# Attention heads that take the first half of the sequence before the second, in a one-core decoder block

## The chip, the core and the metric

The kernel runs on one core of a Trainium2 chip. Its engines have queues of their own and wait for each other by semaphores: TensorE (PE, with its weight loads shown as PEld), VectorE (DVE), ScalarE (ACT), GpSimd (POOL) and SyncE (SP), which here only issues DMAs. The metric is the time of one execution on the device in microseconds; less is better.

## The reference

One layer, sequence 1024, width 1024, all float32. Two token mixers share one input projection; their outputs are gated, added and projected, and a SwiGLU channel mixer follows.

```python
h = rms_norm(x, attn_norm_w)
q, k, v, u, g = split(h @ w_in)             # 1024 + 1024 + 1024 + 2048 + 2048 columns
q, k = rms_norm(q per 64), rms_norm(k per 64)   # 8 heads, two halves of 64 each
# per head, blocks of 128 rows of q:
p = softmax(q1 k1^T / 8 + bias, causal) - lam * softmax(q2 k2^T / 8 + bias, causal)
a = rms_norm(p @ v, subln_w) * (1 - lam_init)
c = silu(layer_norm(causal_conv31(u_a * sigmoid(u_b))))
x = x + (sigmoid(g_a) * (a @ w_proj_attn) + sigmoid(g_b) * (c @ w_proj_conv)) @ w_out
x = x + (silu(gate(rms_norm(x))) * up(rms_norm(x))) @ w_down
```

## The kernel before

Every float32 product is made of three passes (`mm3`, L168 to L170): each operand is split into a rounded part (`hi`, a cast on ACT, L120) and a rest (`lo`, a subtraction on DVE, L125). The kernel runs in stages: the opening with the first projections, the rest of the `u` projections (with the convolution's taps started on DVE), attention, the two output projections, `w_out`, and the channel mixer.

The change lies in **attention**, and in the step that makes q and k for it.

`q_item(h)` projects q and k of head h. It does so in two halves of the sequence, `b` = 0 for rows 0 to 511 and `b` = 1 for rows 512 to 1023. For each half two groups of 48 matmuls fill a PSUM bank each (`pg`), ACT copies them and sums the squares, DVE scales them; later `turn_qk` transposes the half (tile `pQ`, L815), splits it into parts (`ks`, `klo`, `qs`) and moves 64 partitions about with small DMAs on SP (L826 to L837). Each turn waits in the list `late` with a number, `free`: the step before which it may not run, since its buffers are still read.

Attention is a loop over 64 **steps** (h, i): head h, row block i of 128 queries. `ORDER` gives the row blocks' order in a head. A step does this:

- `scores(h, i)`: block i needs (i+1)*128 keys. For each of the two softmaxes PE makes score tiles `sc` of at most 512 keys (L1289, L1290; three PSUM buffers). DVE adds the bias `tb` and finds the minimum (L1291), which frees the buffer; ACT takes the exponential with its sum (L1296); DVE combines the two softmaxes into one tile `E` (L1303 to L1306). Block 7 therefore costs eight times block 0.
- `more`: one group of other work for PE, from `fill`: the projections of the next head's q and k ("Q", four groups a head) and of the gates ("G", two groups each), 24 matmuls of 512 columns or 48 of 256. This is what PE does while DVE and ACT work on the scores. In heads with six groups, two steps have none.
- `turn` of the step before: PE transposes `E` (tile `pT`, L1328), ACT and DVE split it into `ph`, `pl`.
- `slot`: after each second block, `weigh` multiplies by v (tile `pW`, `vh`, `vl`), `back` and `subln` finish the rows (tiles `pB`, `an`, `pS`), and turns of q and k that are due run.
- the convolution's remaining taps (L594, about 1.26 us each on DVE), dealt out by a rough estimate of how much longer PE is busy in a step than DVE (`slack_of`); the last two steps get none of it.

The bias tile `tb` and the v tiles have one buffer each. `tb` of the next head is loaded when the last scores of a head have been read (L869), v of the next head when its last `weigh` has run (L1265).

After the scores of the last step three groups of G are left, which stand over the end of attention: the last `turn`, `weigh`, `back`, `subln`, and the reloading of finished heads (`early`, L1492) for the projection of the attention output, which follows with `aT_hi`, `aT_lo` as its operands.

The instructions of each engine are not issued in the order in which they are written: a scheduler moves them, within rules such as `after(...)`, so that groups of other work come early where it expects PE to wait. `more` lets a group come at most about three steps early.

Of the kernel before, what the change touches and what calls it, by code (L numbers as in the profile page):

```python
# [19 lines left out]
H = 8  # L20
# [11 lines left out]
NT = S // P  # L32
# [25 lines left out]
def kernel(  # L58
# [53 lines left out]
    def nm(s):  # L112
        uid[0] += 1
        return f"{s}_{uid[0]}"

    def f32(ap):
        return ap.bitcast(F32)
# [36 lines left out]
    def pg():  # L154
        npg[0] += 1
        p_, tag = pgs[npg[0] % len(pgs)]
        return p_.tile([P, 512], F32, tag=tag, name=nm("pg"))
# [4 lines left out]
    def pm(z="pm"):  # L162
        npm[0] += 1
        p_, tag = pms[npm[0] % len(pms)]
        return p_.tile([P, 512], F32, tag=tag, name=nm(z))
# [86 lines left out]
    def pcol(key, k=0):  # L252
        c = col[key] + k
        return pvec[:, c : c + 1]
# [121 lines left out]
    def gemm_N(o, halves, shi, slo, i):  # L376

        ts = slice(i * P, (i + 1) * P)
        for k in range(NKT):
            whi, wlo = halves[k // 4]  # L380
            mm3(o, kt(shi, k)[:, ts], kt(slo, k)[:, ts], whi[:, k % 4, :], wlo[:, k % 4, :], k == 0, k == NKT - 1)
# [298 lines left out]
    def rstd_of(ss, n, scale, fast=False):  # L680
        v = sm.tile([P, 16], F32, tag="v", name=nm("v"))[:, :n]
        dve.tensor_scalar(v, ss, scale, EPS, op0=ALU.mult, op1=ALU.add)
        return rsq(v, n, fast)
# [102 lines left out]
    def q_item(h):  # L786
        halves = [ws.next(), ws.next()]
        t = {}
        T[h] = t
        for b in (1, 0):  # L790
            raw = qkp.tile([P, 4, 256], F32, tag="qkraw", name=nm("qkraw"), bufs=2)
            ss = sm.tile([P, 16], F32, tag="ss16", name=nm("ss16"))
            for i2 in range(2):
                o = pg()
                for e in range(2):
                    gemm_N(o[:, 256 * e : 256 * (e + 1)], halves, hT_hi, hT_lo, 4 * b + 2 * i2 + e)
                act.copy(raw[:, 2 * i2 : 2 * i2 + 2, :], o[:].rearrange("p (e c) -> p e c", c=256))
                jk = sm.tile([P, VD], F32, tag="jk", name=nm("jk"), bufs=1)[:, :HD]
                for g in range(8):
                    act.activation(  # L800
                        jk, o[:, g * HD : (g + 1) * HD], AF.Square, accum_out=ss[:, 8 * i2 + g : 8 * i2 + g + 1]
                    )
                if i2 == 0:
                    yield
            r = rstd_of(ss[:], 16, 1.0 / HD, fast=h > 0)
            r4 = raw[:].rearrange("p i (g d) -> p (i g) d", d=HD)
            dve.tensor_tensor(r4, r4, r.unsqueeze(2).to_broadcast([P, 16, HD]), op=ALU.mult)

            def turn_qk(z, key, b, raw):


                dma = nc.sync.dma_start
                pt = pm("pQ")
                for i in range(4):
                    pe.transpose(pt[:, i * P : (i + 1) * P], raw[:, i, z * P : (z + 1) * P], ident[:])  # L815
                w = pcol(key + "n")

                def part(j):
                    return qkp.tile([P, 512], F32R, tag=f"{key}s{j}", name=f"{key}s{j}_{h}_{b}", bufs=2 if key == "q" else 3)

                s1, s2 = part(1), part(2)
                act.activation(s1[:], pt[:], AF.Identity, scale=w)
                lo = part(3) if key == "q" else qkp.tile([P, 512], F32R, tag="klo", name=f"klo_{h}_{b}", bufs=1)
                dve.scalar_tensor_tensor(lo[:], pt[:], w, f32(s1[:]), op0=ALU.mult, op1=ALU.subtract)
                if key == "q":
                    dma(f32(s2[HD:, :]), f32(s1[HD:, :]))  # L826
                    lo2 = part(4)
                    for one, two in ((s1, s2), (lo, lo2)):
                        if one is lo:
                            dma(f32(two[HD:, :]), f32(one[HD:, :]))  # L830
                        dma(f32(two[:HD, :]), f32(one[HD:, :]))
                        dma(f32(one[HD:, :]), f32(one[:HD, :]))
                    t["q", b] = (s1, lo), (s2, lo2)
                else:
                    act.activation(s2[HD:, :], pt[HD:, :], AF.Identity, scale=w[HD:, :])
                    dma(f32(s2[:HD, :]), f32(lo[HD:, :]))
                    dma(f32(s1[HD:, :]), f32(lo[:HD, :]))  # L837
                    t["k", b] = s1, s2

            for z, key in ((1, "k"), (0, "q")):
                free = NT * (h - 1) + (0 if key == "k" and b else NT if key == "q" and not b else NT // 2)
                late.append((free if h else 0, lambda a_=(z, key, b, raw): turn_qk(*a_)))
            yield

    inatt = [False]
    MAKE = {"V": v_item, "U": u_item, "Q": q_item, "G": g_item}

    def run(items):  # L850
# [410 lines left out]
    def load_v(h):  # L1261
        vh = aps.tile([P, NT, VD], F32R, tag="vh", name=f"vh{h}", bufs=1)
        vl = aps.tile([P, NT, VD], F32R, tag="vl", name=f"vl{h}", bufs=1)
        for dst, src in ((vh, v_hi[h // 2]), (vl, v_lo[h // 2])):
            nc.sync.dma_start(  # L1265
                f32(dst[:]),
                src[:, (h % 2) * VD : (h % 2 + 1) * VD].rearrange("(k p) d -> p k d", p=P),
            )
        V[h] = vh, vl
# [37 lines left out]
        ES[h, i] = E[0]  # L1307


    ORDER = [(4, 5, 6, 7, 0, 1, 2, 3)] * (H - 1) + [(6, 7, 4, 5, 2, 3, 0, 1)]  # L1310

    def turn(h, i):

# [19 lines left out]
    def weigh(h, b):  # L1333

        ph, pl = PT.pop((h, b))
        vh, vl = V[h]
        o = pm("pW")
        nkt = 2 * b + 2
        for k in range(nkt):
            mm3(o[:, :256], vh[:, k, :], vl[:, k, :], ph[:, k, :], pl[:, k, :], k == 0, k == nkt - 1)  # L1340
        ar = aps.tile([P, 256], F32, tag="ar", name=nm("ar"), bufs=1)
        act.copy(ar[:], o[:, :256])
        return ar

    def back(h, b, ar):
        pt = pm("pB")
        for e in range(2):
            pe.transpose(pt[:, e * P : (e + 1) * P], ar[:, e * P : (e + 1) * P], ident[:])
        if h not in AN:
            AN[h] = aps.tile([P, NT, VD], F32, tag="an", name=f"an{h}", bufs=1)  # L1350
            SSA[h] = sm.tile([P, NT], F32, tag="ssa", name=nm("ssa"))
        jk = sm.tile([P, VD], F32, tag="jk", name=nm("jk"), bufs=1)
        for e in range(2):
            i = 2 * b + e
            src, r = pt[:, e * P : (e + 1) * P], RL[h][:, i, 0:1]
            act.activation(AN[h][:, i, :], src, AF.Identity, scale=r)
            act.activation(jk[:], src, AF.Square, scale=r, accum_out=SSA[h][:, i : i + 1])

    def subln(h):
        an = AN[h]  # L1360
        r = rstd_of(SSA[h][:], NT, 1.0 / VD, fast=True)
        dve.tensor_tensor(an[:], an[:], r.unsqueeze(2).to_broadcast([P, NT, VD]), op=ALU.mult)
# [23 lines left out]
    load_v(0)  # L1386
    steps = [(h, i) for h in range(H) for i in ORDER[h]]
    scm, weighs, backs, sublns = [], [], [], []
# [22 lines left out]
    def slot(n, nq):  # L1411

        with after(last_fill[0]):
            for h, b, ar in ready(backs, n):
                back(h, b, ar)
                if b == ORDER[h][-1] // 2:
                    subln(h)
# [6 lines left out]
            for h, b in ready(weighs, n):  # L1424
                backs.append((n + 2, (h, b, weigh(h, b))))
                if b == ORDER[h][-1] // 2 and h + 1 < H:
                    load_v(h + 1)
# [365 lines left out]
    for z, (z_, b_, s_, (l, c), full) in enumerate(WSEVEN):  # L1793
# [65 lines left out]
        for i in range(4):  # L1859
            t_ = 4 * l + i  # L1860
            h = xa[t_][:, TOK[c]]
# [273 lines left out]
```

## Time and profile before

| | |
|---|---|
| median of 3 runs | 1727.62 us (1727.13 to 1728.29) |
| profiled execution: time | 1735.99 us |
| profiled execution: span | 1734.2 us |
| PE, DVE, ACT, POOL busy | 99%, 74%, 50%, 13% of the span |
| first score matmul of attention | at 315.08 us of the span |

The profile comes from one execution, some 0.5% slower than the median. "Busy" counts a matmul until it has left the pipeline, so that matmuls overlap: the step from one start to the next is shorter than the duration shown. Times in the timeline and in the chain of waits are microseconds from the start of the span; L numbers are lines of the kernel.

### The profile page before, as it was taken

To read this page: it belongs to the slowest core of one execution; us is meant where nothing else is said; L and a number is where in the kernel's file an instruction comes from. 1 tells how busy PE (TensorE), PEld (TensorE's weight loads), DVE (VectorE), ACT (ScalarE), POOL (GpSimd) and SP (SyncE) were. 2 spreads that over 40 slices of the span, in tenths; PEclk is the share of its full clock that TensorE was granted. 3 is DMA by queue.
4 is the path that set the end of the run, shared out by engine and by line. 5 is a ranking of instruction groups with operands and counts; after the bars stand their busy time and mean duration, and the time that the engine had idled before them with its cause. 6 is when DMAs were issued, how large, how long until landed. Compare 5 with 4: busy or idle time off the path is not lost.

```text
span 1734.2 us, 25866 instructions
## 1 busy us (share of the span) xinstructions
PE 1718.1 (99%) x9245; PEld 1480.7 (85%) x9245; DVE 1286.8 (74%) x2128; ACT 862.0 (50%) x1958; POOL 219.1 (13%) x207
## 2 busy tenths in 40 slices
PE   9899999999999999999999999999999999999999
PEld 7897889998998998988788888888888888888887
DVE  6785889898988888978587768966676667565554
ACT  5234334667777776755557324633333333333332
POOL 3988761000000000000000000000000000000000
PEclk9999999999999999999999999999999999999999
DMA  6244436436335444434973674235445444598663
GB/s 207 80 134 129 151 109 173 122 86 180 108 103 169 114 127 126 116 114 132 333 262 110 212 266 142 78 114 172 153 162 174 154 149 154 172 361 283 218 216 131
DMA packets 261603, 281.64 MB, mean 162 GB/s; under 512 B 16545, under 2 KB 181985, under 8 KB 261474
## 3 DMA queue, kind: packets, MB, share of 16 engines
q1 hardware_dynamic: 255360, 269.28, 48.1%
q0 software_dynamic: 5680, 9.39, 2.7%
q8 instruction: 73, 1.20, 0.3%
q10 hardware_dynamic: 434, 1.32, 0.2%
q14 instruction: 56, 0.46, 0.1%
HBM read 181.84 MB, written 85.50 MB: 154 GB/s over the span
## 4 chain that ended last, share of the span: by engine, by line
PE 94%; DVE 3%; DMA 2%; ACT 1%; issue 1%; SPq 0%; DVEq 0%; ACTq 0%
PE acc L980 30%; PE acc L488 12%; PE pg L168 12%; PE pg L169 12%; PE pg L170 12%; PE wo L1850 4%; PE sc L1289 2%; PE sc L1290 2%; PE pT L1328 2%; DVE acc L594 1%; PE pg L1106 1%; PE pW L168 1%; PE pW L169 1%; PE pW L170 1%; PE pQ L815 1%
## 5 line engine op out<-in xcount | busy, mean ns | idle before, releaser
L594 DVE SCALAR_TENSOR_TENSOR acc<-u,cw,acc 128x1023 f32<-128x1023 f32 (+14 forms) x240 | 303.4, 1264 | 25.2 <-ACT acc L588 22.6
L169 PE MATMUL pg<-wlo,hT_hi 128*128 128x256 f32 x704 | 200.9, 286 | 5.0 <-DVE wlo L125 5.0
L170 PE MATMUL pg<-whi,hT_lo 128*128 128x256 f32 x704 | 201.4, 286 | 0.0
L168 PE MATMUL pg<-whi,hT_hi 128*128 128x256 f32 x704 | 200.8, 286 | 0.4 <-DVE v L125 0.4
L125 DVE TENSOR_TENSOR wlo<-draw,whi 128x1024 fp32r<-128x1024 f32 x75 | 91.8, 1223 | 85.0 <-ACT whi L120 79.9
L120 ACT CAST whi<-draw 128x1024 fp32r<-128x1024 f32 x75 | 79.1, 1055 | 129.5 <-PE acc L488 116.0
L169 PEld LDWEIGHTS pg<-wlo,hT_hi 128*128 128x128 f32 x704 | 135.5, 192 | 7.3 <-DVE wlo L125 5.6
L168 PEld LDWEIGHTS pg<-whi,hT_hi 128*128 128x128 f32 x704 | 135.2, 193 | 2.1 <-DVE v L125 0.6
L170 PEld LDWEIGHTS pg<-whi,hT_lo 128*128 128x128 f32 x704 | 135.5, 192 | 1.7
L120 ACT CAST whi<-wraw 128x1024 fp32r<-128x1024 f32 x90 | 94.6, 1052 | 80.0 <-PE pg L169 31.1
L488 PE MATMUL acc<-wlo,whi 128*128 128x512 f32 x308 | 119.8, 389 | 0.0
L488 PE MATMUL acc<-whi,wlo 128*128 128x512 f32 x308 | 119.8, 389 | 0.0
L1296 ACT ACTIVATE E<-E,mn 128x640 f32<-128x640 f32 (+7 forms) x128 | 99.8, 781 | 30.5 <-DVE mn L1291 28.9
L168 PE MATMUL pg<-hT_hi,whi 128*128 128x512 f32 x288 | 114.4, 397 | 0.1
L169 PE MATMUL pg<-hT_lo,whi 128*128 128x512 f32 x288 | 113.7, 395 | 0.0
L170 PE MATMUL pg<-hT_hi,wlo 128*128 128x512 f32 x288 | 113.7, 395 | 0.0
L120 ACT CAST whi<-s 128x1024 fp32r<-128x1024 f32 x54 | 56.8, 1053 | 104.7 <-PE acc L980 101.7
L125 DVE TENSOR_TENSOR wlo<-wraw,whi 128x1024 fp32r<-128x1024 f32 x75 | 94.6, 1264 | 11.4 <-ACT whi L120 11.2
L1291 DVE CUSTOM_DVE_ANT_0 E<-sc,tb 128x512 f32<-128x512 f32 (+3 forms) x128 | 74.2, 585 | 33.3 <-PE pT L1328 16.0
L980 PE MATMUL acc<-h_hi,whi 128*128 128x512 f32 x240 | 93.4, 389 | 0.0
L980 PE MATMUL acc<-h_lo,whi 128*128 128x512 f32 x240 | 93.4, 389 | 0.0
L980 PE MATMUL acc<-h_hi,wlo 128*128 128x512 f32 x240 | 90.1, 389 | 0.0
(370 smaller groups left out, 4599.6 us busy)
## 6 DMA issues: line engine op xcount, KB each, us to landing
wraw<-in_w_gate_up_dram SPq DMA_DIRECT2D x44, 512.0 KB, 4.8
wraw<-in_w_in_dram SPq DMA_DIRECT2D x40, 512.0 KB, 4.1
qs<-qs SPq DMA_DIRECT2D x96, 128.0 KB, 2.3
wd<-in_w_down_dram SPq DMA_DIRECT2D x44, 256.0 KB, 3.2
tdT<-wd SPq DMA_DIRECT2D x88, 128.0 KB, 4.6
draw<-sdS SPq DMA_DIRECT2D x44, 256.0 KB, 3.8
draw<-tdT SPq DMA_DIRECT2D x44, 256.0 KB, 3.9
wraw<-in_w_in_dram SPq DMA_DIRECT2D x32, 256.0 KB, 3.3
```

What stands on the lines that cost most here:

```text
L120: act.copy(dst, src)
L125: last_lo[0] = dve.tensor_tensor(dst, src, f32(hi), op=ALU.subtract).ins
L168: pe.matmul(o, lh, rh, start=start, stop=False)
L169: pe.matmul(o, lh, rl, start=False, stop=False)
L170: last_mm[0] = pe.matmul(o, ll, rh, start=False, stop=stop).ins
L488: m = pe.matmul(o[s_][i][:], l_[:, ts], r_[:, 512:], start=start and j + y_ == 0, stop=j == n - 1 and y_ == 2, skip_group_check=not start,)
L594: dve.scalar_tensor_tensor(a_, us[c][:, : S - n], cw[:, c, t : t + 1], a_, op0=ALU.mult, op1=ALU.add)
L980: last_mm[0] = pe.matmul(o[:], a_[x_][:, k, :], b_[y_][:, k, :], start=start and k + x_ + y_ == 0, stop=k == 3 and x_ == 1, skip_group_che ...
L1289: pe.matmul(o[:, :w], qh[:, qs], k, start=True, stop=False)
L1291: dve.tensor_tensor_reduce(e[:, ks], o[:, :w], tb[:, S - nk + c0 : S - nk + c0 + w], 1.0, mn[:, j : j + 1] if c0 else 3.0e38, ALU.add, ALU ...
L1296: act.activation(e[:, :nk], e[:, :nk], AF.Exp, bias=mn[:, j : j + 1], scale=-1.0, accum_out=l[:, j : j + 1])
L1850: last_mm[0] = pe.matmul(o[s_][i][:], A[u_], B[v_], start=start and j + y_ == 0, stop=j == 3 and y_ == 2, skip_group_check=not start,).ins
```

## The change

In each head the first half of the sequence is now projected and turned first, and the row blocks run 0 to 7 where they ran 4, 5, 6, 7, 0, 1, 2, 3. In the last head the order was 6, 7, 4, 5, 2, 3, 0, 1 and is now 0, 1, 2, 3, 6, 7, 4, 5. The numbers in `late` follow: k of the first half may be turned from the start of the head before, q of the first half from its middle, k and q of the second half only at the start of their own head.

```diff
-        for b in (1, 0):
+        for b in range(2):
...
-                free = NT * (h - 1) + (0 if key == "k" and b else NT if key == "q" and not b else NT // 2)
+                free = NT * (h - 1) + (NT if b else 0 if key == "k" else NT // 2)
...
-    ORDER = [(4, 5, 6, 7, 0, 1, 2, 3)] * (H - 1) + [(6, 7, 4, 5, 2, 3, 0, 1)]
+    ORDER = [tuple(range(NT))] * (H - 1) + [(0, 1, 2, 3, 6, 7, 4, 5)]
```

The number of matmuls stays at 9232, and every engine does the same operations; what changes is the order, on all engines, from the projection of head 0's q and k to the end of attention. Three places follow.

**PE, near the end of attention, before.** The tiles are scores of block 5 of the last head (`sc`, its key parts of 512 and 256), transposes of block 7 (`pT`), and a group of G (`pg`), here in the middle of the blocks 6, 7, 4, 5 that open this head.

```order
L1328 MATMUL pT_1366_9302<-ident_78,E_1339_9171 128x128 x4
L1328 MATMUL pT_1367_9309<-ident_78,E_1339_9171 128x128 x4
L1289 MATMUL sc_1379_9371<-ks1_7_1_8631,qs1_7_1_8840 128x256
L1348 MATMUL pB_1368_9316<-ident_78,ar_1336_9162 128x128 x2
L1290 MATMUL sc_1379_9371<-ks1_7_1_8631,qs3_7_1_8843 128x256
L168 MATMUL pg_1420_9566<-hT_hi_324,whi_1327_9085 128x512
L169 MATMUL pg_1420_9566<-hT_lo_325,whi_1327_9085 128x512
L170 MATMUL pg_1420_9566<-hT_hi_324,wlo_1328_9086 128x512
L168 MATMUL pg_1420_9566<-hT_hi_324,whi_1327_9085 128x512
L1289 MATMUL sc_1381_9377<-ks2_7_0_8858,qs2_7_1_8841 128x512
```

**PE, the end of attention, now.** The same blocks close the head; the tiles are scores of blocks 4 and 5 and transposes of blocks 6 and 7.

```order
L1289 MATMUL sc_1424_9560<-ks2_7_0_8594,qs2_7_1_9118 128x512
L1290 MATMUL sc_1424_9560<-ks2_7_0_8594,qs4_7_1_9123 128x512
L1328 MATMUL pT_1416_9530<-ident_78,E_1385_9381 128x128 x4
L1328 MATMUL pT_1417_9537<-ident_78,E_1385_9381 128x128 x3
L1289 MATMUL sc_1425_9564<-ks2_7_1_9105,qs2_7_1_9118 128x128
L1290 MATMUL sc_1425_9564<-ks2_7_1_9105,qs4_7_1_9123 128x128
L1289 MATMUL sc_1441_9659<-ks1_7_0_8593,qs1_7_1_9117 128x512
L1290 MATMUL sc_1441_9659<-ks1_7_0_8593,qs3_7_1_9120 128x512
L1328 MATMUL pT_1432_9607<-ident_78,E_1405_9474 128x128 x4
L1289 MATMUL sc_1442_9663<-ks1_7_1_9104,qs1_7_1_9117 128x256
L1290 MATMUL sc_1442_9663<-ks1_7_1_9104,qs3_7_1_9120 128x256
L1328 MATMUL pT_1433_9614<-ident_78,E_1405_9474 128x128 x4
```

Between the scores of these blocks no group `pg` is left: the last one before them ends ahead of the second key part of block 6's second softmax (`sc_1390`), and the next one comes behind the last score tile (`sc_1445`).

**DVE, the same place, now.** Score tiles (L1291 with its reading of the minimum), the combining of blocks 6 and 7 (L1306), the `pl` parts of block 6 and a tap.

```order
L1291 ISA E_1420_9549,mn_1418_9547<-sc_1421_9550,tb7_9022 128x512
L1291 ISA mn_1418_9547 128x1
L1304 SCALAR_TENSOR_TENSOR rl_1411_9494<-rl1_7_9038,neglam_110,l_1404_9473 128x1
L1291 ISA E_1420_9549,mn_1418_9547<-sc_1422_9554,tb7_9022,mn_1418_9547 128x128
L1291 ISA mn_1418_9547 128x1
L1306 SCALAR_TENSOR_TENSOR E_1405_9474<-E_1408_9484,rl_1411_9494,E_1405_9474 128x1024
L1291 ISA E_1423_9559,mn_1418_9547<-sc_1424_9560,tb7_9022 128x512
L1291 ISA mn_1418_9547 128x1
L125 TENSOR_TENSOR pl_1415_9527<-pT_1416_9530,ph_1414_9526 128x4x128
L125 TENSOR_TENSOR pl_1415_9527<-pT_1417_9537,ph_1414_9526 128x3x128
L594 SCALAR_TENSOR_TENSOR acc7_8028<-u7_6145,cw_109,acc7_8028 128x996
```

Before, the rows that close DVE's part of attention are those of blocks 2, 3, 0 and 1, whose scores are at most 512 wide in one tile.

**SP, from head 0 to head 1.** Before, the loads of head 1's v (`vh1`, `vl1`) stand among the DMAs of q of head 1, first half of the sequence:

```order
L826 DMA qs2_1_0_4079<-qs1_1_0_4078 64x512
L831 DMA qs2_1_0_4079<-qs1_1_0_4078 64x512
L1265 DMA vh1_4105<-v_hi0_113 128x8x128
L832 DMA qs1_1_0_4078<-qs1_1_0_4078 64x512
L830 DMA qs4_1_0_4084<-qs3_1_0_4081 64x512
L831 DMA qs4_1_0_4084<-qs3_1_0_4081 64x512
L1265 DMA vl1_4106<-v_lo0_117 128x8x128
```

Now they stand among those of q and k of the second half, which are turned in the same slot:

```order
L836 DMA ks2_1_1_4045<-klo_1_1_4047 64x512
L837 DMA ks1_1_1_4044<-klo_1_1_4047 64x512
L1265 DMA vh1_4096<-v_hi0_113 128x8x128
L826 DMA qs2_1_1_4058<-qs1_1_1_4057 64x512
L831 DMA qs2_1_1_4058<-qs1_1_1_4057 64x512
L830 DMA qs4_1_1_4063<-qs3_1_1_4060 64x512
L831 DMA qs4_1_1_4063<-qs3_1_1_4060 64x512
L1265 DMA vl1_4097<-v_lo0_117 128x8x128
```

Four small DMAs stand between the two loads, where three did. On PE, two score matmuls, five transposes and 30 matmuls of another group now stand between the last product with head 0's v and the first with `vh1`, and 16 more matmuls of that group before the first with `vl1`; before, several groups stood there.

## The prediction

> **What bounds the kernel now.** The page's first part comes first, then the chain of waits by line, then busy time in the attention stage and in its last 24 us.
>
> ```profile
> PE 1718.1 (99%) x9245; PEld 1480.7 (85%) x9245; DVE 1286.8 (74%) x2128; ACT 862.0 (50%) x1958; POOL 219.1 (13%) x207
> PE 94%; DVE 3%; DMA 2%; ACT 1%; issue 1%; SPq 0%; DVEq 0%; ACTq 0%
> 314.00:824.00 510.00, 507.42 (x3389) 464.04 (x3388) 438.48 (x973) 361.02 (x1194) 18.21 (x71) 1.00 0.43 123
> 800.00:824.00 24.00, 23.68 (x136) 20.13 (x135) 19.51 (x43) 13.93 (x42) 0.72 (x4) 1.00 0.35 119
> ```
>
> PE sets the time: 94% of the chain, and in attention (314 to 824 us) it is busy for 507.4 of 510 us. DVE is second there with 438 of 510 us, or 86%. So the change can gain little, at most what PE waits, and it can lose wherever DVE's share rises above PE's for longer than three score buffers carry. PE's waits from 300 to 860 us, by releaser, and the three longest that lie in attention:
>
> ```profile
> PE sc L1289 <- DMA ks<-klo: 1.5, 2, 1.2
> PE sc L1289 <- DVE mn L1291: 0.6, 1, 0.6
> PE pg L168 <- DVE gt L1640: 0.5, 1, 0.5
> PE pg L168 <- ACT sgg L639: 0.4, 1, 0.4
> PE pg L168 <- DVE v L125: 0.4, 1, 0.4
> 323.77 0.50 PE L1289 MATMUL sc<-ks,qs 128*128 128x512 f32 x1 [0.60 <-DVE mn L1291]
> 381.02 0.47 PE L1289 MATMUL sc<-ks,qs 128*128 128x512 f32 x1 [0.30 <-DMA ks<-klo]
> 569.12 0.47 PE L1289 MATMUL sc<-ks,qs 128*128 128x512 f32 x1 [1.22 <-DMA ks<-klo]
> ```
>
> That is 3.4 us in all. The kernel is almost fully packed here, and no reordering takes more than these waits away.
>
> **Part 1, the waits that go: -2.1 us.** The 0.30 and 1.22 us are the first block of heads 1 and 4 waiting for k of the first half, which was turned in the middle of the head before and had only 8 to 12 us of PE work behind it. Now what is turned last before its first use is k and q of the second half, with 9 to 20 us of PE work between transposes and first score, so these two should go. The 0.60 us at 323.77 comes from wide blocks at the very start, while DVE waited for the convolution's accumulator; blocks 0 and 1 take less than a third of that, and the scores of block 3 come only after some 6 us of other work. Together 0.30 + 1.22 + 0.60 = 2.1 us. The waits on `gt`, `sgg` and `v` lie outside the moved stretch or do not depend on the block order, and stay.
>
> **Part 2, the end of attention: +5.5 us.** Before, blocks 2, 3, 0, 1 closed the last head; now 6, 7, 4, 5 do, and the scheduler has spent the groups of other work ahead of them. From the last score matmul of `sc_1390` to that of `sc_1444` no group stands on PE. So I sum both engines' work between these points. DVE's prices are steps from one start to the next, since an operation starts some 0.08 us before the end shown of the one before it:
>
> ```profile
> 783.47 0.69 DVE L125 TENSOR_TENSOR pl<-pT,ph 128x512 fp32r<-128x512 f32 x1
> 784.07 0.68 DVE L1291 CUSTOM_DVE_ANT_0 E<-sc,tb 128x512 f32<-128x512 f32 x1
> 784.68 0.55 DVE L125 TENSOR_TENSOR pl<-pT,ph 128x384 fp32r<-128x384 f32 x1
> 785.15 1.25 DVE L594 SCALAR_TENSOR_TENSOR acc<-u,cw,acc 128x1004 f32<-128x1004 f32 x1
> 786.32 0.34 DVE L1291 CUSTOM_DVE_ANT_0 E<-sc,tb,mn 128x128 f32<-128x128 f32 x1
> 786.59 0.08 DVE L1291 DVE_READ_ACCUMULATOR2_ANT mn<- 128x1 f32 x1
> L1291 DVE CUSTOM_DVE_ANT_0 E<-sc,tb,mn 128x512 f32<-128x512 f32 x16 | 11.9, 742 | 0.0
> L1291 DVE CUSTOM_DVE_ANT_0 E<-sc,tb,mn 128x384 f32<-128x384 f32 x16 | 9.8, 611 | 2.1 <-PE sc L1290 2.0
> L1306 DVE SCALAR_TENSOR_TENSOR E<-E,rl,E 128x1024 f32<-128x1024 f32 x8 | 10.2, 1280 | 0.1
> L1306 DVE SCALAR_TENSOR_TENSOR E<-E,rl,E 128x896 f32<-128x896 f32 x8 | 9.2, 1145 | 0.0
> L1303 DVE RECIPROCAL rl<-l 128x2 f32<-128x2 f32 x64 | 10.2, 160 | 16.0 <-ACT E L1296 15.6
> L1304 DVE SCALAR_TENSOR_TENSOR rl<-rl,neglam,l 128x1 f32<-128x1 f32 x64 | 13.7, 214 | 0.5
> ```
>
> In the new order DVE must do, before the buffer that `sc_1444` needs is free (the one of `sc_1425`): five score parts of 512 at 0.61, two second parts of 512 at 0.66, one of 384 at 0.53, two of 128 at 0.26, two `pl` of 512 at 0.60 and one of 384 at 0.47, three taps at 1.17, the combining of block 7 at 1.20 and of block 6 at 1.07, and two pairs of small ones at 0.08 + 0.13. That is 3.05 + 1.32 + 0.53 + 0.52 + 1.20 + 0.47 + 3.51 + 2.27 + 0.42 = 13.3 us. PE's prices come from long runs in the chain:
>
> ```profile
> 20.66 2.87 PE pg L1106 x24
> 364.62 0.87 PE pT L1328 x8
> 1140.97 371.73 PE acc L980 x1640
> ```
>
> A matmul of 512 columns takes 0.227 us, of 256 0.120, of 128 0.109. In the same stretch PE has 14 of 512 (3.17), 2 + 12 of 256 (1.67), 4 of 128 (0.44) and 23 transposes (2.50): 7.8 us. So PE waits 13.3 - 7.8 = 5.5 us, in pieces of 1 to 2 us at one score tile after the other. Before, the closing blocks ran in the 24 us shown above with PE busy for 23.68. The bounds: three score buffers let DVE lag by up to three parts, 1.8 us, which the count through `sc_1425` already holds, and an error of a tenth in DVE's prices is 1.3 us, so 4.0 from below; from above, ACT's exponentials stand in DVE's path (DVE waited 15.6 us on them over all 64 blocks, 0.24 each), so 6.5. What hides nothing here is that the three groups of G left behind the scores cannot come forward: PE takes its queue in order.
>
> **Part 3, v loaded closer to its use: +1.5 us.** Because a head now ends with its longest blocks and the next one opens with its shortest, less PE work lies between the last product with one head's v and the first with the next.
>
> ```profile
> DMA to landing us min/median/max: 3.7/5.2/11.4
> 392.46 0.37 SPq L1265 DMA_DIRECT2D vh<-v_hi  x1
> 394.94 0.53 SPq L1265 DMA_DIRECT2D vl<-v_lo  x1
> ```
>
> The first row is that of all 16 v loads. From head 0 to 1 PE now has 30 matmuls of 256, two scores and five transposes: 3.6 + 0.45 + 0.55 = 4.6 us until `vh1`, and 18 matmuls of 256 more, 6.8 us, until `vl1`. `vh1` lands 5.2 us after its issue: 0.6 us of waiting. `vl1` goes out some 2.5 us later, as the two SP rows of this head show with three DMAs between them, and lands at 2.5 + 5.2 = 7.7, when PE stands at 6.8 + 0.6: 0.3 more, and with a fourth DMA in between 0.5. So 1.0 us, from 0 (landing in 3.7) to 7.1 (11.4). At the other six changes of head the same count of the new order gives 10 to 16 us of PE work, against loads that leave up to 3 us late, behind small DMAs that wait for each other: they fit with a median landing, and I take 0.5 us for all six, between 0 and 3.
>
> **Part 4, behind the last scores: +0.5 us.** ACT's new order casts the third reloaded head (`aTh2`) ahead of evacuating a group of G and ahead of the last `ph`. These are such a load in the chain, and a cast of the same size:
>
> ```profile
> 824.02 7.30 DMA early<-a_d
> L120 ACT CAST whi<-draw 128x1024 fp32r<-128x1024 f32 x75 | 79.1, 1055 | 129.5 <-PE acc L488 116.0
> ```
>
> The load can leave only when block 4's transposes have freed a buffer, and from there to the last `pW`, which needs that `ph`, PE has 5.4 us of other work. With 7.3 us for the load and 1.1 for the cast it would cost 3.0 us, with the shortest v landing, 3.7, nothing. The last products need only their last two key blocks from it, so I take 0.5, from 0 to 3.
>
> The rest moves at no cost by the same counts: `E` has at least 2 us in hand at every transpose but those of part 2, because groups stand between; if they did not, each block's exponential and combining, 2 to 4 us, would show. `tb` of the next head now has 2.3 to 4.9 us of DVE work as cover where it had 3.8 to 7.8; DVE's extra waiting of 1 to 3 us a head meets 3.5 us or more in hand at the score buffers.
>
> **The sum.** -2.1 + 5.5 + 1.5 + 0.5 = +5.4 us. The profiled execution took 1735.99 us with a span of 1734.2, the median of the runs is 8.4 us less; I add the difference to both: 1741.4 profiled, and **1733.0 us** as the median. A measurement of this kernel can tell about 0.2% from no change, 3.5 us, so between 1724.2 and 1731.1 is "same".
>
> **The rivals.**
>
> *Only the end of attention counts.* v lands in time and part 4 is hidden: -2.1 + 5.5 = +3.4, 1731.0, and with part 2 at its lower bound 1729.5. For it speaks the 3.7 us landing, against it the 2.5 us between the issues of the two halves. Chance 0.16, all of it "same".
>
> *The clock drops too.* A long wait of PE early in the kernel, and the stretch behind it with its granted clock third from the end:
>
> ```profile
> 70.41 0.39 PE L169 MATMUL pg<-wlo,hT_hi 128*128 128x256 f32 x1 [4.17 <-DVE wlo L125]
> 70.95:77.75 6.80, 6.00 (x29) 5.71 (x28) 3.32 (x2) 1.04 (x1) 6.80 (x3) 0.50 0.65 191
> ```
>
> PE waited 4.17 us at once and then ran at half clock for 6.8 us. If the 5.5 us of part 2, spread over 13 us, or a late v has the same effect once, half of 6.8 us is lost more: +8.8, 1736.4. Waits of 1.22 us left the clock at 1.00, and the single waits here are 2 us at most; hence 0.12. [...]
>
> *v lands late everywhere.* With landings of 7 us and more at three or four heads, part 3 becomes some 5 us: +9, 1736.6. Chance 0.08.
>
> *Faster.* The removed waits count and nothing takes their place: 1725.5 for the 2.1 us, 1724 with the 1.3 us of other waits. The place is DVE before `sc_1390`: it would have to be 5.5 us ahead of PE there, and it can be ahead of no score that PE has not made, three tiles or 1.8 us. Below 1724.2, where "faster" begins, all waits of the stage would have to go. Chance 0.04.
>
> **The numbers.** Forecast (+3.5 to +9 without the clock) 0.60, clock 0.12, late v 0.08, end alone 0.16, faster 0.04. Slower by over 0.2% is 0.60 + 0.12 + 0.08 = 0.80, within 0.2% 0.16, faster 0.04. The range takes part 2 at 4.0 with nothing else added (+1.9, 1729.5) as its low end, and at the high end parts 2 to 4 near their tops or the clock on a fuller sum (+12, 1739.6): 1729.0 to 1740.0. It leaves out the faster case and the longest landings.
>
> **What would show it.** In the new profile the end of attention should have two or three slices of 5 us with PE busy about half and DVE all of the time, PE waiting on L1291; a PE wait at the first `pW` of head 1, on `vh` or `vl`; no wait on `ks<-klo`; the clock at 1.00 throughout. I would be wrong if PE stayed above 95% from the last group to the last score, or if its waits sat at the starts of heads on `tb` or at the `pT` of blocks 4 to 7 in the middle heads, which I count at nothing.

## The result: 11.7 us slower

| | before | after |
|---|---|---|
| median of 5 runs | 1727.62 us | 1739.33 us |
| lowest to highest | 1726.92 to 1728.95 us | 1737.28 to 1740.20 us |
| ratio, 95% interval | | 1.0065, 1.005 to 1.008 |
| profiled execution: span | 1734.2 us | 1736.7 us |

The forecast was 1733.0 us, with a range of 1729 to 1740. The direction and the range held; of the 11.7 us only 5.4 were in the sum.

The two profiles differ by 2.5 us only, since the profiled execution of the old kernel met an event in its opening that 12 of the 14 profiled executions here do not have: the wait of 4.17 us and the half clock behind it that the prediction shows. The same window of both kernels, the old one first (length, then busy time of PE, its weight loads, DVE, ACT and POOL, the granted clock third from the end):

```profile
40.00:80.00 40.00, 35.04 (x224) 32.16 (x223) 29.37 (x20) 8.98 (x13) 39.24 (x17) 0.91 0.22 70
```

```profile
40.00:80.00 40.00, 40.00 (x291) 37.65 (x290) 24.29 (x27) 12.59 (x17) 40.00 (x17) 1.00 0.29 98
```

The old kernel's first matmul of line 980 starts at 101.75 us, the new one's at 93.89. Taking these 7.9 us off, the profiles differ by 10.4 us, near the 11.7 of the medians. The event is no property of the old kernel: a later variant of the new kernel (`e12_gaps_gate_casts`) had the same wait in its profiled execution, 1740.48 us against 1735.4 to 1735.7 in its other runs.

The page of the new kernel, its chain by engine, and PE's longest waits from 300 to 860 us (in all, times, longest):

```profile
PE 1719.0 (99%) x9245; PEld 1481.4 (85%) x9245; DVE 1279.7 (74%) x2128; ACT 858.9 (49%) x1958; POOL 219.0 (13%) x207
...
PE 92%; DVE 3%; ACT 2%; DMA 2%; issue 1%; SPq 0%; DVEq 0%
```

```profile
PE sc L1289 <- DVE mn L1291: 2.2, 3, 1.3
PE pW L168 <- ACT ph L120: 1.8, 1, 1.8
PE pg L168 <- ACT jk L800: 1.8, 1, 1.8
PE pT L1328 <- DVE E L1306: 0.7, 1, 0.7
PE pT L1328 <- ACT E L1296: 0.6, 1, 0.6
```

Both traces record 9245 matmuls (the text above counts 9232), so PE's work is the same before and after.

The waits for `ks<-klo` are gone, and none for `vh` or `vl` has come. The new ones lie in three places, shown here by windows, with the half clock that follows two of them:

```profile
380.00:387.00 7.00, 5.26 (x38) 4.26 (x36) 5.92 (x15) 6.94 (x31) 0.96 (x3) 1.00 0.40 103
387.01:393.83 6.82, 6.03 (x28) 6.03 (x29) 6.20 (x17) 4.98 (x29) 0.00 (x0) 0.50 1.00 267
793.18:806.84 13.66, 9.79 (x55) 6.90 (x54) 13.61 (x33) 10.89 (x30) 0.36 (x2) 1.00 0.13 49
823.91:827.33 3.42, 1.25 (x7) 1.05 (x8) 1.56 (x2) 2.98 (x9) 0.00 (x0) 1.00 1.02 351
827.33:830.74 3.41, 3.41 (x9) 2.63 (x9) 2.04 (x2) 3.38 (x5) 0.00 (x0) 0.50 0.41 141
```

To size them I add up how much later each matmul starts after the one before it than its full-clock price allows (0.227 us for 512 columns, 0.172 for 384, 0.119 for 256, 0.109 for 128). From 300 to 860 us this gives 11.4 us for the old kernel and 20.7 for the new:

| place in the new kernel | waits | half clock | together |
|---|---|---|---|
| change from head 0 to head 1, 380 to 394.5 us | 3.1 | 2.8 | 5.9 |
| end of attention, 790 to 806.5 us | 6.0 | - | 6.0 |
| last `pW`, 823 to 831 us | 2.7 | 1.6 | 4.3 |
| everything else (old kernel: all of its 11.4) | | | 4.4 |

So three places cost 16.2 us, and elsewhere 7.0 us went: 9.2 of the 10.4.

**The first place** was in no part of the forecast. DVE, ACT and PE there, in the new kernel's timeline (start, duration; in brackets the idle time before and what ended it):

```profile
372.37 0.17 DVE L1303 RECIPROCAL rl<-l 128x2 f32<-128x2 f32 x1 [2.00 <-ACT E L1296]
...
372.83 1.28 DVE L1306 SCALAR_TENSOR_TENSOR E<-E,rl,E 128x1024 f32<-128x1024 f32 x1
...
374.50 1.25 DVE L594 SCALAR_TENSOR_TENSOR acc<-u,cw,acc 128x999 f32<-128x999 f32 x1
...
376.27 0.28 DVE L1291 CUSTOM_DVE_ANT_0 E<-sc,tb 128x128 f32<-128x128 f32 x1
...
376.59 0.40 ACT L1296 ACTIVATE E<-E,mn 128x128 f32<-128x128 f32 x1 [3.12 <-DVE mn L1291]
...
381.09 0.24 ACT L800 ACTIVATE jk<-pg 128x64 f32<-128x64 f32 x1
...
387.37 0.29 ACT L800 ACTIVATE jk<-pg 128x64 f32<-128x64 f32 x1
...
387.80 0.58 PE L168 MATMUL pg<-whi,hT_hi 128*128 128x256 f32 x1 [1.78 <-ACT jk L800]
```

Head 0 now ends with its longest block, and DVE has its combining, two `pl` and a tap to do before the first score of head 1. It had itself stood for 2.00 us, for an exponential of that block which ACT began only at 371.11 us, behind seven squares of the Q group before. ACT has the exponential of head 1's first score at the head of its queue: it stands for 3.12 us, until 376.59, with the eight squares of a Q group behind it whose last matmul had started at 367.96. Then exponentials, the turned `ks` and `qs` and the squares share ACT, and the eighth square ends at 387.76. PE needs that group's PSUM buffer for the next Q group.

**The second place** is part 2. DVE has work all the time there (13.61 of 13.66 us in the third window), from `sc_1390`'s bias step, the first row, to the end of the one that frees the buffer for `sc_1444`; PE's wait for that follows, and then the first matmul of the next group:

```profile
792.66 0.61 DVE L1291 CUSTOM_DVE_ANT_0 E<-sc,tb,mn 128x384 f32<-128x384 f32 x1
...
806.06 0.35 DVE L1291 CUSTOM_DVE_ANT_0 E<-sc,tb,mn 128x128 f32<-128x128 f32 x1
...
806.20 0.50 PE L1289 MATMUL sc<-ks,qs 128*128 128x512 f32 x1 [1.27 <-DVE mn L1291]
...
807.12 0.40 PE L168 MATMUL pg<-hT_hi,whi 128*128 128x512 f32 x1
```

ACT's last cast of weights ahead of that group ended at 784.40 us, DVE's last subtraction for them at 785.66, and ACT had emptied the buffer of the group before it by 792.04. So it was ready behind the score that waited, and PE ran it only after that: in this trace PE kept to the order of its queue, as the forecast had it.

**The third place** is part 4. The load that ACT's cast waits for, in the chain of waits (start, duration), and then the timeline with what stood behind the cast:

```profile
817.02 6.73 DMA early<-a_d
```

```profile
823.77 1.04 ACT L120 CAST aTh<-early 128x1024 fp32r<-128x1024 f32 x1 [4.34 <-DMA early<-a_d]
824.72 0.68 ACT L639 ACTIVATE sgg<-pg,pvec 128x512 f32<-128x512 f32 x1
...
825.30 0.36 ACT L120 CAST ph<-pT 128x256 fp32r<-128x256 f32 x1
...
825.72 0.38 PE L168 MATMUL pW<-ph,vh 128*128 128x256 f32 x1 [1.83 <-ACT ph L120]
```

### The profile page after: what moved, and what is told of

Read it like the earlier page. It is cut to its first block, busy times and chain, and to the rows that moved or that the text cites. A ratio compares the mean times of both kernels' runs of the same rounds, so it can differ in the third digit from the quotient of the medians.

```text
span 1736.7 us, 25821 instructions
## 1 busy us (share of the span) xinstructions
PE 1719.0 (99%) x9245; PEld 1481.4 (85%) x9245; DVE 1279.7 (74%) x2128; ACT 858.9 (49%) x1958; POOL 219.0 (13%) x207
## 4 chain that ended last, share of the span: by engine, by line
PE 92%; DVE 3%; ACT 2%; DMA 2%; issue 1%; SPq 0%; DVEq 0%
PE acc L980 30%; PE acc L488 12%; PE pg L168 12%; PE pg L169 12%; PE pg L170 12%; PE wo L1850 3%; PE sc L1290 2%; PE sc L1289 2%; DVE acc L594 2%; PE pT L1328 2%; PE pg L1106 1%; PE pW L169 1%; PE pW L170 1%; PE pW L168 1%; PE pQ L815 1%
## 5 line engine op out<-in xcount | busy, mean ns | idle before, releaser
L1296 ACT ACTIVATE E<-E,mn 128x256 f32<-128x256 f32 (+7 forms) x128 | 100.0, 781 | 37.7 <-DVE mn L1291 37.5
L1291 DVE CUSTOM_DVE_ANT_0 E<-sc,tb 128x512 f32<-128x512 f32 (+3 forms) x128 | 73.5, 586 | 20.4 <-PE sc L1290 7.8
```

What stands on the lines that cost most here:

```text
L1291: dve.tensor_tensor_reduce(e[:, ks], o[:, :w], tb[:, S - nk + c0 : S - nk + c0 + w], 1.0, mn[:, j : j + 1] if c0 else 3.0e38, ALU.add, ALU ...
L1296: act.activation(e[:, :nk], e[:, :nk], AF.Exp, bias=mn[:, j : j + 1], scale=-1.0, accum_out=l[:, j : j + 1])
```

## The experiments

Times are medians; the old kernel beside them ran at 1727.3 to 1728.0 us, and the ratios are to it.

### The early casts held back, `e3_casts_behind`

```diff
     with after(last_of(mybir.EngineType.Activation)):
         early_split(0)
         early_split(1)
-    early(4)
-    for h in range(2, 5):
-        early_split(h)
+        early(4)
+        for h in range(2, 5):
+            early_split(h)
```

> The changed kernel, with the casts of the reloaded heads 2 to 4 held behind ACT's last evacuation of a pW tile, so that they cannot stand ahead of the last ph. Theory: the wait of 2.6 us at the last pW goes, and with it the half clock from 827.3 to 830.7 us, which costs 1.6 us: 1739.3 - 4.2 = 1735.1 us. Rival 1, the half clock is not due to this wait but to the whole end of attention: only 2.6 us go, 1736.7. Rival 2, the loads or casts that now come later are waited for by the projection that follows: no gain, 1739 or more.

Measured: 1734.87 us, 1.0036 (1.0025 to 1.0047). The wait at the last `pW` and the half clock behind it are both gone, so part 4 with its clock is 4.5 us by the medians; by the sum over the matmuls it is 4.2.

### A gate group first, `e4_gate_first`

```diff
-        ["Q2", "G2", "G3"],
+        ["G2", "Q2", "G3"],
```

> The changed kernel, with one group of the gates exchanged for q and k of the next head at the start of head 1 (G2, Q2, G3 where Q2, G2, G3 stood), so that no two groups of Q follow each other while ACT's queue holds the first exponentials of head 1. Theory: PE's waits at 384 to 388 us come from ACT's sixteen squares of a Q group, which stand behind an exponential that waited 3.1 us for DVE, and hold the PSUM buffer of the next Q group; they cost 3.0 us, and the half clock after them (387.0 to 393.8 us) 2.7 us: 1739.3 - 5.7 = 1733.6 us. Rival 1, clock and wait are two things and the clock stays low: 1736.4. Rival 2, the place waits for v of head 1 or for its bias tile, and the group only hid it: 1739, with the wait at the first pW.

Measured: 1733.61 us, 1.0032 (1.0021 to 1.0044). No wait is left between 380 and 395 us; PE's waits for `jk` fall from 1.8 us to 0.2:

```profile
PE pT L1328 <- DVE E L1306: 1.8, 2, 1.4
PE pW L169 <- DVE pl L125: 1.1, 2, 0.9
...
PE pg L168 <- ACT jk L800: 0.2, 1, 0.2
PE pW L168 <- DMA vh<-v_hi: 0.2, 1, 0.2
```

So it was the squares that PE waited for. That v would have cost nothing without them is not shown. The edit also puts more PE work between the last product with head 0's v and the first with `vh1`, 9.3 us where the changed kernel has 4.6. In the changed kernel the second half of v came only just in time:

```profile
386.80 0.54 SPq L1265 DMA_DIRECT2D vl<-v_lo  x1
vl<-v_lo SPq DMA_DIRECT2D x1, 512.0 KB, 9.0
396.28 0.28 PE L170 MATMUL pW<-ph,vl 128*128 128x256 f32 x1
```

It landed 9.0 us after its issue, at 395.8, half a microsecond before its first product. With the 6.8 us of PE work that the forecast counts, and none of the other lost time, PE would have stood at that product at about 390.5 and waited some 5 us. That is an estimate, which takes the landing as unchanged; no run removes the wait for the squares and leaves this cover as it was.

The 5.7 us of the medians are also a balance of several places: in this trace head 1 loses 0.2 us instead of 6.0, the wait at the last `pW` is down from 2.7 to 1.2 us, and 1.5 us more are lost between 475 and 770 us. The runs of this kernel spread from 1731.4 to 1736.7 us. Its profile has a half clock at the end of attention (800.3 to 803.7 us) after 4.1 us of waits, and the profile of the changed kernel has none there after 6.0 us of waits. The last section comes back to this.

### The new last head alone in the old kernel, `e2_tail_alone`

```diff
-        for b in (1, 0):
+        bs = (0, 1) if h == H - 1 else (1, 0)
+        for b in bs:
...
-                free = NT * (h - 1) + (0 if key == "k" and b else NT if key == "q" and not b else NT // 2)
+                free = NT * (h - 1) + (0 if key == "k" and b == bs[0] else NT if key == "q" and b == bs[1] else NT // 2)
...
-    ORDER = [(4, 5, 6, 7, 0, 1, 2, 3)] * (H - 1) + [(6, 7, 4, 5, 2, 3, 0, 1)]
+    ORDER = [(4, 5, 6, 7, 0, 1, 2, 3)] * (H - 1) + [(0, 1, 2, 3, 6, 7, 4, 5)]
```

> The old kernel with the new last head alone: heads 0 to 6 as before (4, 5, 6, 7, 0, 1, 2, 3), the last one 0, 1, 2, 3, 6, 7, 4, 5, with q and k of that head projected first half first. In its order ACT's cast of the third reloaded head stands behind the last ph, so part 4 is absent. Theory: the old kernel plus the end of attention, 5.9 us, less nothing: 1733.5 us against 1727.6. If the clock halves at the end as well, 1735 to 1737. Rival, the end of attention costs what it does only because heads 0 to 6 feed it late: 1728 to 1729.

Measured: 1725.85 us, 0.9985 (0.9975 to 0.9994): not 5.9 us slower but some 2 us faster. The blocks 6, 7, 4, 5 close attention here too, and the end of attention is packed:

```profile
780.00:799.00 19.00, 19.00 (x109) 16.33 (x108) 17.55 (x36) 12.71 (x27) 0.36 (x2) 1.00 0.27 97
```

In its trace 42 matmuls of G (a group has 24) stand among the scores behind those of block 6; in the changed kernel none does. The closing blocks alone, with these groups among them, cost nothing.

### An end with short blocks, `e1_light_end`

```diff
-    ORDER = [tuple(range(NT))] * (H - 1) + [(0, 1, 2, 3, 6, 7, 4, 5)]
+    ORDER = [tuple(range(NT))] * (H - 1) + [(2, 3, 6, 7, 4, 5, 0, 1)]
```

> The changed kernel, but its last head runs 2, 3, 6, 7, 4, 5, 0, 1, so that attention ends with its two shortest blocks. Theory: in the changed kernel's trace the end of attention holds 6.0 us more than the pure PE work (790 to 806 us), and the wait behind the last scores with the half clock after it 4.3 us (823 to 831 us). Both come from closing with blocks 4 and 5, so both should go, against some 1 us of small waits that the old kernel also has there: about 9 us off 1739.3, 1730 us. Rival 1, only the 5.5 us of DVE work that I forecast for the end come back and ACT's early cast still stands ahead of the last ph: 1734. Rival 2, the loss lies in the middle heads: 1737 or more.

Measured: 1736.96 us, 1.0045 (1.003 to 1.0061), a miss. The end and the cast cost little now, but the blocks 6 and 7 brought their waits with them to 775 to 783 us, this time on DMAs, and the clock was at half from 780.05 to 786.88:

```profile
PE sc L1289 <- DMA qs<-qs: 2.9, 2, 2.3
PE pW L168 <- DMA vh<-v_hi: 1.7, 1, 1.7
PE pS L1369 <- DVE t L655: 1.1, 1, 1.1
PE pW L170 <- DMA vl<-v_lo: 1.0, 1, 1.0
```

The heavy blocks of the last head follow two steps behind the heavy blocks of head 6 here, so the load of v and the turned q have little PE work to hide behind: 2.5 us stand between the last product with head 6's v and the first with head 7's, where the changed kernel has 10.5.

### No taps in the last six steps, `e5_no_taps_end`

```diff
-    slack[-2:] = [0.0, 0.0]
+    slack[-6:] = [0.0] * 6
```

> The changed kernel, with none of the convolution's taps dealt into the last six steps (two steps before), so that they fall on earlier ones. In the order three taps leave DVE's stretch between the second key part of block 6 and the last score tile, and 14 matmuls of a group stay in that stretch. Theory, DVE is the bound there: its 13.3 us fall by three taps of 1.17 us, and PE's 7.8 us rise: the 5.9 us of waits at the end go to 2 or less, 1739.3 - 4 to 6 = 1734 us. Rival 1, the end waits for ACT's exponentials or for the score buffers' latency, and taps only fill DVE's own waits: 1738 to 1739. Rival 2, the taps dealt to earlier steps cost there what they save here: 1739.

Measured: 1733.60 us, 1.0037 (1.0024 to 1.005). With less of DVE's work in that stretch PE is busy:

```profile
790.00:806.00 16.00, 15.90 (x97) 13.48 (x96) 12.60 (x32) 12.41 (x31) 0.36 (x2) 1.00 0.52 132
```

So DVE was the bound there. The edit changed the order too, though: part of a group now stands among the closing scores, so the run does not part fewer taps from more PE work. The wait behind the early cast is gone here too. The saving of 5.7 us is less than the two together, in part since the wait for the squares at head 1, with taps now dealt to earlier steps, grew from 1.8 to 3.2 us.

### Groups held back, `e6_groups_held`

```diff
-        with after(scm[-4] if len(scm) >= 4 else None):
+        with after(scm[-2 if n > len(steps) - 5 else -4] if len(scm) >= 4 else None):
```

> The changed kernel, with the groups of the last four steps allowed only one step early instead of three. The block order and the instructions are the same; two groups move to a place behind scores of block 7 and into the end. The old kernel with the new last head (1725.9 us) had two groups there and none of the waits. Theory, it is not the closing blocks but that their groups were spent ahead of them: the 5.9 us at the end go, the early cast stays: 1739.3 - 5.9 = 1733.4 us. Rival, DVE cannot follow PE here and the waits only move ahead of the groups: 1739.

Measured: 1741.46 us, 1.0082 (1.0066 to 1.0097), as the rival said, and 2 us more. The end keeps less than half of its waits, but PE now waits at 780 to 787 us, and the clock is at half from 783.8 to 790.6 us:

```profile
781.17 0.52 PE L1328 MATMUL pT<-ident,E 128*128 128x128 f32 x3 [1.04 <-DVE pl L125]
...
784.31 0.55 PE L168 MATMUL pW<-ph,vh 128*128 128x256 f32 x1 [1.58 <-DMA vh<-v_hi]
...
786.56 0.69 PE L1289 MATMUL sc<-ks,qs 128*128 128x384 f32 x1 [0.47 <-DVE mn L1291]
```

So the groups that were spent early had covered real waits. This points to a want of PE work in the whole stretch from the heavy blocks of head 6 to the end, not in the last 14 us alone. With the two other edits this hold gives the same picture:

> The changed kernel with three edits together: the early casts held behind the last evacuation, the gate group ahead of q and k at head 1, and the groups of the last four steps held. Measured alone, the first two gave 4.5 and 5.7 us. Theory, the three losses are independent and are all there is: 1739.3 - 4.5 - 5.7 - 5.9 = 1723.2 us, 4 to 5 us below the old kernel, that is, the new order of the heads is better by the waits that go. Rival, the old order has an advantage of its own in the middle heads: 1728 or more.

Measured for `e8_all_three`: 1734.53 us, 1.0043 (1.0027 to 1.0059). Head 1 and the last `pW` are clean, but 5.4 us of waits and a half clock from 778.5 to 785.3 us stand at the first blocks 6 and 7.

### The steps without a group, `e11_gaps_light` and `e15_old_gaps_heavy`

In heads with six groups (2, 4 and 6) two positions have none. Those were blocks 0 and 2, and by the change became blocks 4 and 6. The edit moves them back to the light blocks:

```diff
-        return 0 if plan[n // NT] == 6 and n % NT in (4, 6) or n == len(steps) - 1 else 1
+        return 0 if plan[n // NT] == 6 and n % NT in (0, 2) or n == len(steps) - 1 else 1
```

> The changed kernel, with the two steps that have no group, in heads with six groups, at the positions 0 and 2 of the head where they were 4 and 6. In the old order the positions 4 and 6 are blocks 0 and 2, the light ones; in the new order they are blocks 4 and 6, so that the group is missing where DVE has the most to do. With this edit the groups of head 6 come with its heavy blocks, fewer are spent ahead, and two stand in the end of attention again. Theory, this table of positions, which the change left as it was, causes the loss at the end: 5.9 us go, the early cast stays: 1739.3 - 5.9 = 1733.4 us. Rival, the closing blocks themselves cost it, and holding back groups only moves the waits, as the run with groups held has shown: 1739 or more.

Measured: 1741.70 us, 1.0082 (1.0067 to 1.0097). The end is packed, as the theory said:

```profile
790.00:806.00 16.00, 16.00 (x95) 13.74 (x93) 14.94 (x30) 11.27 (x24) 0.36 (x2) 1.00 0.28 93
```

But other places paid more than that:

```profile
PE pW L168 <- DMA vh<-v_hi: 5.0, 1, 5.0
PE pW L168 <- ACT ph L120: 3.0, 1, 3.0
PE pg L168 <- ACT sgg L639: 2.8, 1, 2.8
```

The 3.0 us are the early cast, the 2.8 us a wait for ACT at 402.9 us, in head 1. The 5.0 us are the v of head 2: without a group at the first block of the head only 3.2 us of PE work stand between the last product with the old v and the first with the new, where the changed kernel has 11.5 and the old one 19.3 (prices above, summed over the order). That is the mechanism of part 3, at another head.

The mirror puts the same edit into the old kernel, where it empties the heavy blocks 4 and 6:

> The mirror: the old kernel with its steps without a group at positions 0 and 2 of a head, which in its order are the heavy blocks 4 and 6. Theory, the missing groups at heavy blocks cost PE time wherever they are: the old kernel loses some 3 to 9 us, 1731 to 1736, with waits on DVE at the scores of heavy blocks of heads 5 to 7. Rival, the table is of no account and it is the order alone: 1727 to 1728.

Measured: 1731.36 us, 1.0019 (1.001 to 1.0029). The edit costs the old kernel 3.7 us by the medians, at the low end of the expectation, but not where the expectation had it. Of the added waits in its trace one is DVE's at the score of a heavy block (1.05 us, at the start of head 6); the others are 0.99 and 0.66 us for the squares in heads 2 and 4, and the longest wait for `ks` has moved from head 4 to head 2. So the mirror bears the theory out in part only.

### Three edits, `e12_gaps_gate_casts` and `e16_gaps_head6`

> The changed kernel with three edits: the steps without a group at positions 0 and 2, the gate group ahead of q and k at head 1, the early casts behind the last evacuation. Theory, these are the three losses: 1739.3 - 5.9 - 5.7 - 4.5 = 1723.2 us, below the old kernel by the waits that the new order takes away and a few small ones. Rival, the waits of the end move ahead to blocks 6 and 7, as with groups held: 1734.

Measured: 1735.68 us, 1.0054 (1.0039 to 1.0069). The end, the cast and head 1's squares are clean, but at the change to head 2 PE waits 3.8 us for q, whose transposes stand only some 5.5 us of PE work ahead of its first score:

```profile
PE sc L1289 <- DMA qs<-qs: 4.1, 2, 3.8
PE pW L170 <- DMA vl<-v_lo: 1.1, 2, 0.8
```

The last run moves the positions in head 6 alone, with the other two edits as before:

```diff
-        return 0 if plan[n // NT] == 6 and n % NT in (4, 6) or n == len(steps) - 1 else 1
+        return 0 if plan[n // NT] == 6 and n % NT in ((0, 2) if n // NT == 6 else (4, 6)) or n == len(steps) - 1 else 1
```

> The changed kernel with the gate group ahead of q and k at head 1, the early casts behind the last evacuation, and the two steps without a group moved to positions 0 and 2 in head 6 alone. With the positions moved in all heads (1735.7 us) the end of attention had no wait left, but the changes to heads 1 and 2 got new ones: 3.7 us of PE work stood between the last product with one v and the first with the next, and PE waited up to 5 us for v or for the small DMAs of q. In the order of this kernel that distance is 8.0 us or more at every head, and 9 us or more between the transposes of q and its first score. Theory, then no wait of these is left and the three losses go: 1739.3 - 5.9 - 5.7 - 4.5 = 1723 us, below the old kernel (1727.6) and below it with the new last head (1725.9). Rival, each place that is relieved passes its wait on to another change of heads, because DVE and ACT have the same work at the same density: 1728 to 1732.

Measured: 1726.27 us, 0.9994 (0.9985 to 1.0003): 13.1 us below the changed kernel, and level with the old one. All that PE waits for from 300 to 860 us:

```profile
PE sc L1289 <- DVE mn L1291: 1.1, 1, 1.1
PE pg L168 <- DVE gt L1640: 0.5, 1, 0.5
PE pg L168 <- ACT jk L800: 0.4, 1, 0.4
PE pW L170 <- DMA vl<-v_lo: 0.3, 1, 0.3
```

By the sum over the matmuls it loses 7.7 us in this stretch, where the changed kernel loses 20.7: the difference, 13.0, is what the medians show. I had expected 3 us less, from adding the savings of three kernels. In this trace 5.3 us are lost between 475 and 770 us, where the changed kernel loses 2.3: the edits pass some waits on to the middle heads. The old kernel with the new last head (1725.85 us, 7.9 us lost) is the only one that is shown to beat both.

### Spare work in a wait, `e10_spare`

```diff
+        if (h, b) == (0, 3):
+            spare = pm("spare")
+            for e in range(14):
+                pe.transpose(spare[:, :P], ar[:, :P], ident[:])
```

> The changed kernel with 14 transposes of 128 columns into a tile that nothing reads, 1.5 us of PE work, put into PE's queue where it waits 1.95 us at the change from head 0 to head 1. The wait for ACT's squares should end at the same time, so the wait itself is still paid. In five drops of the clock in the traces so far PE had been busy for 12 to 39% of the 3.4 us before each, and at 41% it had not dropped. Theory, the clock drops for want of PE work in that stretch: with the spare work PE is busy for some 75% of it, the clock stays at 1.00 there and 1.2 to 2.7 us come back: 1737 us. Rival 1, the clock drop is not set by this wait: 1739. Rival 2, the spare work delays ACT's evacuations and so the squares: 1740 to 1741.

Measured: 1742.81 us, 1.0088 (1.0072 to 1.0104). It tells nothing of the clock: the spare tile itself waited for its PSUM buffer, so that the transposes ran behind the wait instead of in it, and PE was busy for 24% of the 3.41 us ahead of the drop. It is 3.5 us slower than the changed kernel. The two new terms in its trace are the 1.5 us of transposes and a wait of 1.8 us on DVE's `aTl` behind attention:

```profile
PE pg L168 <- DVE aTl L1378: 1.8, 1, 1.8
...
PE spare L1352 <- DVE pl L125: 1.5, 1, 1.5
```

That the clock would have stayed with PE busy in the wait was therefore not shown by a run; what stands for it is the comparison of windows below.

## Why the forecast was right in direction and short in size

- **Part 1 (-2.1): right.** None of the three waits is in the new trace. With the small ones that went as well, all other places fell from 11.4 to 4.4 us, so 4.9 us more went than the sum has.
- **Part 2 (+5.5): the size was right, the cause too narrow.** DVE took from 792.66 to 806.41 us, 13.75 us where the sum says 13.3, and PE lost 6.0 where it says 5.5. But `e2_tail_alone` closes with the same blocks at no loss. What the forecast read in the order, that no group is left there, belongs to the cause, and it did not ask why none is left. Eight of the last twelve steps are heavy now (blocks 4 to 7 of head 6, then 6, 7, 4, 5), against four in `e2_tail_alone`, and the two steps of head 6 without a group fell on blocks 4 and 6. Fewer taps (`e5`) or those groups at the heavy blocks (`e11`) remove the loss; holding groups back (`e6`) only moves it.
- **Part 3 (+1.5): nothing of it came.** The wait at the first `pW` of head 1, named as a sign, is not there: PE reached `vh1` late, since it had waited for ACT's squares. That is luck, not a better cover: `vl1` took 9.0 us to land, where the sum takes the median of 5.2, and the other loss hid it. The mechanism is real: with 3.2 us of PE work as cover, `e11` waited 5.0 us.
- **Part 4 (+0.5): the term was mis-sized.** The wait was 2.7 us, inside its bound of 3.0, and the clock made it 4.3 with its 1.6. The load took 6.73 us; the row of the same transfer (7.30) stood in the forecast, and the value was taken near a bound from another transfer instead.
- **"The rest moves at no cost": this step failed.** It counted `E`, `tb` and the score buffers, and left out the PSUM buffers of the Q groups, which come free only when ACT has squared them. DVE's extra waiting at a change of heads was held to be covered; it passed through ACT's queue to PE: 3.1 us of waits and 2.8 of clock. Taking the group out of the way (`e4`) gave 5.7 us, with more cover for v in the same edit.
- **The rival "the clock drops too" (0.12) came true**, not through the end of attention or a late v, which the forecast named as candidates, but at the two other places, for 4.4 us in the profile; "clock 1.00 throughout" did not hold. It had been given a low chance since waits of 1.22 us had left the clock at 1.00 and no single wait above 2 us was expected. None came: ahead of the two drops the longest were 1.95 and 1.99 us.
- **The direction held in part by luck.** Without the 5.9 us at head 1 the places add up to 9.2 - 5.9 = 3.3 us, less than the 3.5 us that the forecast takes for no change. The waits that went, 7.0 us, paid for most of the 10.3 us of parts 2 and 4; the sum had counted on 2.1.

## What to carry to other kernels

When blocks are reordered, look at every table and limit that goes by position (here the steps without a group, the taps, three steps of lead): it now speaks of other blocks. Follow an engine's queue past its first wait: what stands behind an instruction that waits, and whose buffer that holds. Take a transfer's price from the row of that transfer, and look at the granted clock behind waits like those of 1.95 and 1.99 us here.

## What the runs showed of the hardware

**The clock fell behind waits of 1.95 and 1.99 us.** In the changed kernel it was at half for 6.83 us from 387.01 us and for 3.41 us from 827.33 us, and in the old kernel's profile for 6.83 us from 70.93 us. Counting each matmul at its full-clock price, PE was busy for 31% of the 3.41 us ahead of the first, 26% ahead of the second and 12% ahead of the third. The longest single waits there were 1.95, 1.99 and 4.17 us. From 803.43 us in the changed kernel, at its end of attention, PE was busy for 40% of as long a window, with no wait above 1.43 us by the same count, and the clock stayed at 1.00 behind it. So PE had not been idle for the whole of any of these windows, and yet the clock fell behind three of the four; what share of busy time is enough to keep it was not shown.

The waits at head 1, alike to 0.01 us in the changed kernel and in `e3_casts_behind`, were followed by 6.83 us at half clock in the one and by 3.41 in the other. So in these two executions the same waits did not cost the same clock, and why was not shown. The spread of `e4_gate_first` (1731.4 to 1736.7 us) may come from the same; that is an estimate, since its single runs were not profiled, and its order at the end of attention differs from the changed kernel's.

**ACT's queue carried a wait a long way.** ACT stood 3.12 us until 376.59, and PE paid for it 11 us later, with 1.78 us at 387.80. Behind the exponential that was not ready stood eight squares whose input was ready at 368 us; ACT ran the first of them at 381.09 and the last at 387.37.
